# Queries of heads 0 to 13 computed with the keys and values, gates one head late, weight scaling on GpSimd

## The chip, the cores and the metric

The kernel runs on one core of a Trainium2 chip. The metric is the device time of one execution in microseconds (us). A core has a matrix engine (TensorE, PE in the profile; its weight loads are PEld), three engines that work element by element on 128 partitions (VectorE = DVE, ScalarE = ACT, GpSimd = POOL), a sync engine (SP) that issues most of the transfers, 16 DMA engines, an on-chip memory (SBUF) and the accumulators of TensorE (PSUM, eight banks here).

## The reference, cut to what matters

One inference step of an encoder over 640 tokens: 512 of one new stream, and 16 for each of 8 running streams. Layer A mixes and projects; then come shared keys and values, one layer B of attention, and a last norm. The part that matters, shortened:

```python
hk = rmsnorm(x, norm_kv)
kvf = hk @ w_kv                      # 2048 -> 2048 keys, 2048 values, 16 forget logits
k, v = kvf[..., :2048], kvf[..., 2048:4096]        # 16 heads of 128
h = rmsnorm(x, norm_b)
z = h @ w_in_b                       # 2048 -> 2048 queries, 2048 gates
q, gate = z[..., :2048], z[..., 2048:]
s = einsum(q, k_all) / sqrt(128) + Fq - Fk         # forgetting attention, causal
o = softmax(s) @ v_all
x = x + (o * silu(gate)) @ w_out_b
return rmsnorm(x, norm_f), k, v, ...
```

Both norms divide a row by the same root mean square and differ only in their gain per channel. All is float32; the kernel forms a large product of float32 from three matmuls on a high and a low part of each operand (high with high, high with low, low with high).

## The kernel before, in words

The stream lies transposed in SBUF, channels on partitions and the 640 tokens along the free axis, split into high and low parts.

**First part of layer B, the key and value stage** (`kv_pair`, L1034, called for the list `kvs` of L318). The list has 16 entries (q, m): q is 0 for keys and 1 for values, m counts pairs of heads. `pair8` (L260) computes one entry, 256 output channels, by a scheme that makes four block products out of seven (`ORDER`, L253, `OPER`, L119): over four slabs of weights (one entry of `loads` each, 512 KB) it issues 7 products x 2 x 3 = 42 matmuls of 128x320 a slab, 168 an entry. `advance` (L235) fetches and prepares slabs ahead: `prep` (L208) scales a slab by the norm gain on ScalarE (four instructions, L213), forms sums on VectorE and splits both into high and low. `combine` (L280) puts the seven products together on VectorE, GpSimd multiplies the pair by the row factors `R` (L1050), and `rows_out` (L1017) sends it on, as a generator that `tick` advances at some points of the next entry. Keys are stored transposed to the DRAM scratch `kscr` and row-wise to the output; values go row-wise to the scratch `sv`. The last entry takes its slabs in the order `LAST` and starts `last_blocks` (L1008).

**Second part, the attention loop** (from L1437). `proj` (L1132) computes 128 channels of the queries or gates of one head by eight plain block products for the pair of heads' seven: 16 steps of 6 matmuls of 128x320, 96 in all, on weights that `fetchb` loads in chunks of 256 KB (four a head) and `split_next` (L1110) scales (`scale_next`, L1104, on VectorE at L1107) and splits (L1115 on ScalarE, L1117 on VectorE). Between its steps it calls `step` (L1146), which advances two lists of generators in turn:

- `front` holds `scoring(h)`: transposes of the cached keys on VectorE (L1277), matmuls of scores (L1282 cached keys; L1290 and L1292 to L1294 new keys in four blocks), masks, softmax, and the loads and splits for the next head;
- `back` holds `valuing(h - 1)`: transposes of the probabilities (L105, through L1384 and L1385), products with the values (L1407, L1411, L1420 to L1423), and the output `og`.

`q_block` (L1223) runs `proj`, empties `front`, and writes the query of a head into SBUF (L1229 to L1232, then its split). `gate_block` (L1238) runs `proj`, applies `R` (L1241) and Silu, and hands the gate to `valuing`, which multiplies on GpSimd (L1434). Ahead of the loop stand `q_block(0)` and `q_block(1)`, the latter beside `scoring(0)`. A pass h of the loop, h = 1 to 15, puts `scoring(h)` and `valuing(h - 1)` on the lists and runs `gate_block(h - 1)` and `q_block(h + 1)`; pass 15 has no query block. `valuing(15)` with `gate_block(15)` follows, then the output projection and the last norm.

What sets the order: TensorE runs the matmuls in the order in which the program issues them (`manual_schedule`). The other engines' queues and SP's transfers are ordered by the framework's planner before the run, by its own estimate of when each instruction can go; on the chip each queue then runs in that fixed order, so that an instruction or a transfer that waits holds up all behind it. Every tile has a fixed number of buffers (`bufs`), and a load into a buffer waits for its last reader.

Of the kernel before, what the change touches and what calls it, by code (L numbers as in the profile page):

```python
# [39 lines left out]
def tile_yoco_step(ctx, tc, i, o):  # L40
# [167 lines left out]
    def prep():  # L208
        n = nprep[0]
        raw = loaded.pop(n)  # L210
        if len(loads[n]) > 2:
            for k in range(4):
                nc.scalar.activation(raw[:, k, :], raw[:, k, :], AF.Copy, scale=loads[n][2][:, k : k + 1])  # L213
# [104 lines left out]
    kvs = [(q, m) for m in range(8) for q in range(2)]  # L318
    LAST = (3, 0, 1, 2)
    for q, m in kvs:  # L320
        for s in LAST if (q, m) == kvs[-1] else range(4):
            c0 = q * D + m * 2 * P
            loads.append(("s", wkv[:, 4 * s : 4 * s + 4, c0 : c0 + 2 * P], nkv_c[:, 4 * s : 4 * s + 4]))
# [526 lines left out]
    kscr = [dram.tile([2 * P, NT], F32, name=f"kscr{m}") for m in range(8)]  # L850
    sv = [dram.tile([NT, P], F32, name=f"sv{h}") for h in range(H)]
# [11 lines left out]
    Fs = pv.tile([P, 5, H], F32, name="Fs")  # L863
    Fq, FqS = Fs[:, :4], Fs[:, 4]
# [152 lines left out]
    def rows_out(q, m, t):  # L1017
        yield
        if q == 0:
            store(pair_rows(kscr[m]), t)  # L1020
# [13 lines left out]
    def kv_pair(n, q, m):  # L1034
        def hook(s, j):
            if (n, s) == (0, 0) and j in (3, 6):
                last_forget(j // 6)
                if j == 6:
                    last_rows()
            if (n, s, j) == (15, 2, 0):  # L1040
                last_blocks()

        pp = pair8(hook, LAST if n == 15 else range(4))
# [60 lines left out]
    def scale_next(n):  # L1104
        if len(braws) > n and braws[n][1] is not None:
            r = braws[n][0].rearrange("p (k n) -> p k n", n=P)
            nc.vector.tensor_tensor(r, r, braws[n][1].unsqueeze(2).to_broadcast([P, 4, P]), op=ALU.mult)  # L1107
# [71 lines left out]
    with ExitStack() as ctx2:  # L1179
# [43 lines left out]
        def q_block(h):  # L1223
            pp = proj()
            drain(front)
            qt = pk.tile([P, NP], F32, tag="qt", name="qt")
            qs = pk.tile([P, NS], F32, tag="qs", name="qs")
            sc = float(P) ** -0.5
            nc.vector.scalar_tensor_tensor(qt[:, :HALF], pp[:, 0, :HALF], sc, R[:, :HALF], op0=ALU.mult, op1=ALU.mult)  # L1229
            nc.vector.scalar_tensor_tensor(qt[:, HALF:], pp[:, 1, : NP - HALF], sc, R[:, HALF:NP], op0=ALU.mult,  # L1230
                                           op1=ALU.mult)
            nc.vector.scalar_tensor_tensor(qs, pp[:, 1, NP - HALF : HALF], sc, R[:, NP:], op0=ALU.mult, op1=ALU.mult)  # L1232
            qh = pk.tile([P, NP], F32R, tag="qh", name="qh")
            ql = pk.tile([P, NP], F32R, tag="ql", name="ql")
            split(qh, ql, qt)
            return qt, qh, ql, qs

        def gate_block(h):  # L1238
            pp = proj(16 if h > H - 3 else 10)
# [3 lines left out]
            gates.append(sg)  # L1243
# [22 lines left out]
        cached, gates = {}, []  # L1266
# [3 lines left out]
        def scoring(h, q_):  # L1270
# [41 lines left out]
            qt, qh, ql, qs = q_  # L1312
            if h == 0:
                split_new_keys(0)
            kt, kh, kl = keys[h]
# [25 lines left out]
            nc.tensor.matmul(sn[:, :NS], qs, kt[:, NP:NT], start=True, stop=True)  # L1341
            nc.vector.scalar_tensor_tensor(s2[:, : 2 * PAST], ss, FqS[:, h : h + 1], fs[:, : 2 * PAST], op0=ALU.add,
# [16 lines left out]
            if more:  # L1359
                split_new_keys(h + 1)  # L1360
                load_sums(h + 1)
# [6 lines left out]
        def valuing(h):  # L1368
# [63 lines left out]
            while not gates:  # L1432
                yield
            nc.gpsimd.tensor_tensor(og[:, h, :], og[:, h, :], gates.pop(), op=ALU.mult)  # L1434
# [5 lines left out]
        load_new_keys(0)  # L1440
        load_sums(0)
        load_values(0)
        load_new_values(0)
        q_ = {}
        q_[0] = q_block(0)
        front.append(scoring(0, q_[0]))
        q_[1] = q_block(1)
# [139 lines left out]
```

## Time and profile before

| what | us |
| --- | --- |
| median of 3 runs | 2844.34 |
| lowest and highest | 2841.94, 2845.12 |
| the profiled execution, its own time | 2844.21 |
| its span, first to last instruction | 2842.5 |
| TensorE busy in the span | 2760.4 (97%) |
| VectorE busy | 2019.7 (71%) |
| ScalarE busy | 1151.2 (41%) |
| GpSimd busy | 404.8 (14%) |

The granted TensorE clock has a mean of 0.987 over the span. The span starts with layer A, up to about 1541 us; the key and value stage ends at 1951.7, the attention loop with its tail at about 2607, and the output projection fills the rest. Busy time is a share of the whole span; what an engine bounds is read stage by stage.

### The profile page before, as it was taken

Reading aid. Unit: us, or ns where it says so; the run is one execution under the profiler, and the core shown is the slowest. Engines: PE = TensorE matmul, PEld = TensorE weight load, DVE = VectorE, ACT = ScalarE, POOL = GpSimd, SP = SyncE. Lnnn points to the kernel's source line nnn. Section 1 sums busy time; section 2 is a strip of 40 time slices with the busy share of each in tenths; the row PEclk is TensorE's granted clock in tenths of the full one; section 3 lists DMA queues with packets and bytes.
Section 4 is the critical chain, followed back from the end, with each engine's and each line's share of the span. In section 5 each row is a group of like instructions: output and inputs, shape, how many; then the busy total and the mean of one; then the engine's idle time right before and its main releaser. Section 6 shows DMA issues by size and latency. Waiting matters only on the chain.

```text
span 2842.5 us, 46301 instructions
## 1 busy us (share of the span) xinstructions
PE 2760.4 (97%) x18194; PEld 2649.7 (93%) x18194; DVE 2019.7 (71%) x3415; ACT 1151.2 (41%) x1912; POOL 404.8 (14%) x373
## 2 busy tenths in 40 slices
PE   7899999999999999999998999998999999999998
PEld 7799999999998999999997999998999999998787
DVE  7877778888786858586365988886766766666333
ACT  5443333333333535343234555553434443444222
POOL 2212122232340120202023101111000000000000
PEclk8999999999999999999999999999999999999999
DMA  3344444444335686868642455556565655565832
GB/s 126 109 139 130 134 124 122 140 124 130 118 110 182 174 169 182 175 173 165 177 154 87 109 130 122 136 118 158 138 155 141 150 129 141 140 153 118 130 96 98
DMA packets 647044, 391.36 MB, mean 138 GB/s; under 512 B 322788, under 2 KB 601748, under 8 KB 646696
## 3 DMA queue, kind: packets, MB, share of 16 engines
q1 hardware_dynamic: 627240, 334.64, 44.1%
q0 software_dynamic: 19584, 53.75, 8.8%
q8 instruction: 142, 2.33, 0.3%
q14 instruction: 78, 0.64, 0.1%
HBM read 299.98 MB, written 88.32 MB: 137 GB/s over the span
## 4 chain that ended last, share of the span: by engine, by line
PE 43%; DVE 4%; DMA 2%; ACT 1%; issue 1%; POOL 1%; SPq 0%; DVEq 0%; ACTq 0%; POOLq 0%
PE banks L1086 15%; PE banks L251 9%; PE banks L1479 7%; PE banks L669 5%; PE banks L1407 2%; DVE wl L84 2%; PE banks L1282 1%; DMA raw<-in_w_kv 1%; PE banks L105 1%; ACT wh L81 0%; DMA raw<-in_w_grp_a 0%; PE banks L1422 0%; PE banks L1421 0%; PE banks L1420 0%; PE banks L1292 0%
## 5 line engine op out<-in xcount | busy, mean ns | idle before, releaser
L251 PE MATMUL banks<-b,wh 128*128 128x320 f32 x2688 | 605.1, 312 | 10.4 <-ACT forgot L840 6.6
L251 PE MATMUL banks<-th,wh 128*128 128x320 f32 x1792 | 559.8, 312 | 9.1 <-ACT cve L292 6.2
L251 PE MATMUL banks<-th,wl 128*128 128x320 f32 x1792 | 557.6, 311 | 4.0 <-DVE wl L84 4.0
L251 PE MATMUL banks<-tl,wh 128*128 128x320 f32 x1792 | 557.3, 311 | 0.7 <-DVE tl L84 0.7
L251 PEld LDWEIGHTS banks<-b,wh 128*128 128x128 f32 x2688 | 451.7, 189 | 12.3 <-ACT forgot L840 7.2
L251 PE MATMUL banks<-b,wl 128*128 128x320 f32 x1344 | 417.2, 310 | 0.4 <-DVE wl L84 0.4
L84 DVE TENSOR_TENSOR wl<-raw,wh 128x768 fp32r<-128x768 f32 (+1 forms) x264 | 307.4, 1165 | 145.0 <-ACT wh L81 144.5
L81 ACT ACTIVATE wh<-raw 128x768 fp32r<-128x768 f32 (+1 forms) x264 | 230.6, 875 | 379.9 <-issue 138.2
L81 ACT ACTIVATE wh<-sums 128x1024 fp32r<-128x1024 f32 x224 | 236.2, 1054 | 340.5 <-DVE sums L220 340.1
L1086 PE MATMUL banks<-b,whi 128*128 128x320 f32 x1536 | 355.4, 315 | 0.0
L251 PEld LDWEIGHTS banks<-th,wh 128*128 128x128 f32 x1792 | 339.7, 190 | 11.4 <-ACT cve L292 6.9
L251 PEld LDWEIGHTS banks<-th,wl 128*128 128x128 f32 x1792 | 339.7, 190 | 4.7 <-DVE wl L84 4.7
L251 PEld LDWEIGHTS banks<-tl,wh 128*128 128x128 f32 x1792 | 339.9, 190 | 1.0 <-DVE tl L84 1.0
L84 DVE TENSOR_TENSOR wl<-sums,wh 128x1024 fp32r<-128x1024 f32 x224 | 281.5, 1257 | 59.9 <-ACT wh L81 59.5
L1086 PEld LDWEIGHTS banks<-b,whi 128*128 128x128 f32 x1536 | 254.8, 189 | 1.6 <-issue 0.2
L251 PEld LDWEIGHTS banks<-b,wl 128*128 128x128 f32 x1344 | 253.9, 189 | 0.6 <-DVE wl L84 0.6
L1086 PE MATMUL banks<-b,wlo 128*128 128x320 f32 x768 | 196.1, 310 | 0.0
L217 DVE TENSOR_TENSOR sums<-raw 128x512 f32<-128x512 f32 x236 | 172.4, 730 | 14.6 <-DMA raw<-in_w_out_a 3.5
L1115 ACT ACTIVATE whi<-raw 128x512 fp32r<-128x512 f32 x144 | 90.0, 628 | 151.9 <-PE banks L1086 56.3
L669 PE MATMUL banks<-th,wh 128*128 128x320 f32 x576 | 132.3, 311 | 4.4 <-DVE cve L294 3.9
L1086 PEld LDWEIGHTS banks<-b,wlo 128*128 128x128 f32 x768 | 133.9, 188 | 0.0
L669 PE MATMUL banks<-tl,wh 128*128 128x320 f32 x576 | 131.8, 310 | 0.0
(397 smaller groups left out, 4830.6 us busy)
## 6 DMA issues: line engine op xcount, KB each, us to landing
raw<-in_w_in_a SPq DMA_DIRECT2D x128, 512.0 KB, 4.1
raw<-in_w_out_a SPq DMA_DIRECT2D x64, 512.0 KB, 4.9
raw<-in_w_kv SPq DMA_DIRECT2D x64, 512.0 KB, 3.9
raw<-in_w_in_b SPq DMA_DIRECT2D x128, 256.0 KB, 3.6
raw<-in_w_grp_a SPq DMA_DIRECT2D x32, 512.0 KB, 6.1
kc<-in_cache_k SPq DMA_DIRECT2D x64, 256.0 KB, 4.8
vc<-in_cache_v SPq DMA_DIRECT2D x16, 1024.0 KB, 6.7
raw<-in_w_out_b SPq DMA_DIRECT2D x64, 256.0 KB, 3.3
```

The costliest lines, as they stand in the source:

```text
L81: a = nc.scalar.activation(hi, x, AF.Copy)
L84: nc.vector.tensor_tensor(lo, x, hi.bitcast(F32), op=ALU.subtract)
L105: nc.tensor.transpose(out, x, ident[:n, :n])
L217: nc.vector.tensor_tensor(sums[:, :, 0:2, :], raw[:, :, 1:3, :], raw[:, :, 0:1, :].to_broadcast([P, 2, 2, P]), op=ALU.subtract)
L251: nc.tensor.matmul(bank[:, :HALF], w[kk][:, a, :], x, start=first and q == 0, stop=last and q == 2)
L669: nc.tensor.matmul(bk[s], w, x[:, s * HALF : (s + 1) * HALF], start=k + q == 0, stop=k == 7 and q == 2)
L1086: nc.tensor.matmul(acc_[:, s, :HALF], w, stream(k, q, s), start=f, stop=l)
L1115: nc.scalar.activation(hi, raw, AF.Copy)
L1282: nc.tensor.matmul(sp[rows, b % 2 * PAST : (b % 2 + 1) * PAST], qs[:, rows], kct[:, b * PAST : (b + 1) * PAST], start=True, stop=True)
L1407: nc.tensor.matmul(po[32 * q : 32 * q + 32, :P], pts[:, j, 32 * q : 32 * q + 32], vc[:, 4 * q + j, :], start=(j == 0), stop=False)
L1479: nc.tensor.matmul(out, (ol if q == 2 else oh)[k][:, ts], wl if q == 1 else wh, start=first and q == 0, stop=last and q == 2)
```

## The change

The query products of heads 0 to 13 move from the attention loop into the key and value stage, as seven more entries of `kvs` (q = 2). Their weights come from `w_in_b` and are scaled by a gain that already has the factor 1/sqrt(128) in it (`qgain`). The order at the end of the list becomes keys 6, values 6, keys 7, values 7, queries 6. A query pair takes the path of a key pair up to the factor `R` and goes, transposed, to a new DRAM scratch `qscr`; it has no row-wise output. Heads 14 and 15 keep their plain query blocks, which now stand ahead of the loop beside `scoring(0)`, with 6 steps each, and store to `qscr` as well.

In the loop `load_query(h + 1)` fetches a head's query (320 KB) during `scoring(h)`, and `split_query(h + 1)` splits it after the last score block of head h. A pass has one gate block with 22 steps, after which both lists are emptied; then the gate is taken from PSUM, and VectorE multiplies it into `og`. The scaling of the attention loop's weights goes from VectorE to GpSimd. `step` is called at evenly spread places of `proj`.

```diff
@@ prep
+            gain, k0 = qgain[0] if loads[n][2] == 2 else nkv_c, loads[n][3]
             for k in range(4):
-                nc.scalar.activation(raw[:, k, :], raw[:, k, :], AF.Copy, scale=loads[n][2][:, k : k + 1])
+                nc.scalar.activation(raw[:, k, :], raw[:, k, :], AF.Copy, scale=gain[:, k0 + k : k0 + k + 1])
@@ the list
-    kvs = [(q, m) for m in range(8) for q in range(2)]
+    kvs = [(q, m) for m in range(8) for q in range(3)]
+    kvs = kvs[:20] + kvs[21:23] + kvs[20:21]
+    qgain = []
...
+            loads.append(("s", (wkv, wkv, winb)[q][:, 4 * s : 4 * s + 4, c0 : c0 + 2 * P], q, 4 * s))
...
+    qgain.append(pv.tile([P, KT], F32, name="qg"))
+    nc.vector.tensor_scalar_mul(qgain[0], nb_c, float(P) ** -0.5)
@@ rows_out
-        if q == 0:
-            store(pair_rows(kscr[m]), t)
+        if q != 1:
+            store(pair_rows((kscr if q == 0 else qscr)[m]), t)
+        if q == 2:
+            return
@@ scale_next
-            nc.vector.tensor_tensor(r, r, braws[n][1].unsqueeze(2).to_broadcast([P, 4, P]), op=ALU.mult)
+            nc.gpsimd.tensor_tensor(r, r, braws[n][1].unsqueeze(2).to_broadcast([P, 4, P]), op=ALU.mult)
@@ proj
-                if kk * ticks % KT < ticks:
+                for _ in range((kk + 1) * ticks // KT - kk * ticks // KT):
                     step()
@@ queue of weight chunks
-    queue(winb, 0, nb_c)
-    queue(winb, P, nb_c)
+    for h in (14, 15):
+        queue(winb, h * P, nb_c)
     for h in range(H):
         queue(winb, D + h * P, nb_c)
-        if h < H - 2:
-            queue(winb, (h + 2) * P, nb_c)
@@ attention loop
+        def load_query(h):
+            qt = pk.tile([P, NT], F32, tag="qt", name="qt")
+            dma(qt, qscr[h // 2][h % 2 * P : (h % 2 + 1) * P, :])
+            queries[h] = [qt]
+
+        def split_query(h):
+            qh = pk.tile([P, NP], F32R, tag="qh", name="qh")
+            ql = pk.tile([P, NP], F32R, tag="ql", name="ql")
+            split(qh, ql, queries[h][0][:, :NP])
+            queries[h] += [qh, ql]
+
         def q_block(h):
+            pp = proj(6)
+            qp = pb.tile([P, NT], F32, tag="vt", name="qp")
+            nc.vector.scalar_tensor_tensor(halves(qp), pp[:, :, :HALF], float(P) ** -0.5, halves(R), op0=ALU.mult,
+                                           op1=ALU.mult)
+            dma(qscr[h // 2][h % 2 * P : (h % 2 + 1) * P, :], qp)
 
         def gate_block(h):
-            pp = proj(16 if h > H - 3 else 10)
+            pp = proj(22 if h < H - 1 else 12)
+            drain(front)
+            drain(back)
...
-            gates.append(sg)
+            nc.vector.tensor_tensor(og[:, h, :], og[:, h, :], sg, op=ALU.mult)
@@ scoring
+            if more:
+                load_query(h + 1)
...
                 split_new_keys(h + 1)
+                split_query(h + 1)
                 load_sums(h + 1)
@@ valuing
-            while not gates:
-                yield
-            nc.gpsimd.tensor_tensor(og[:, h, :], og[:, h, :], gates.pop(), op=ALU.mult)
+            finished.append(h)
@@ the loop
-        q_[0] = q_block(0)
-        front.append(scoring(0, q_[0]))
-        q_[1] = q_block(1)
+        front.append(scoring(0))
+        q_block(14)
+        q_block(15)
+        drain(front)
         for h in range(1, H):
-            front.append(scoring(h, q_[h]))
+            front.append(scoring(h))
             back.append(valuing(h - 1))
             gate_block(h - 1)
-            if h < H - 1:
-                q_[h + 1] = q_block(h + 1)
-            drain(front)
-            drain(back)
```

More of the change, by code (lines that the diff above doesn't have):

```diff
@@ L321, in tile_yoco_step @@
         for s in LAST if (q, m) == kvs[-1] else range(4):
-            c0 = q * D + m * 2 * P
-            loads.append(("s", wkv[:, 4 * s : 4 * s + 4, c0 : c0 + 2 * P], nkv_c[:, 4 * s : 4 * s + 4]))
+            c0 = q % 2 * D + m * 2 * P
+            loads.append(("s", (wkv, wkv, winb)[q][:, 4 * s : 4 * s + 4, c0 : c0 + 2 * P], q, 4 * s))
     start = ExitStack()
@@ L850, in tile_yoco_step @@
     kscr = [dram.tile([2 * P, NT], F32, name=f"kscr{m}") for m in range(8)]
+    qscr = [dram.tile([2 * P, NT], F32, name=f"qscr{m}") for m in range(8)]
     sv = [dram.tile([NT, P], F32, name=f"sv{h}") for h in range(H)]
@@ L1039, in hook @@
                     last_rows()
-            if (n, s, j) == (15, 2, 0):
+            if (n, s, j) == (len(kvs) - 1, 2, 0):
                 last_blocks()
-        pp = pair8(hook, LAST if n == 15 else range(4))
+        pp = pair8(hook, LAST if n == len(kvs) - 1 else range(4))
         if n == 0:
@@ L1221, in tile_yoco_step, with q_block @@
         nc.gpsimd.memset(fs[:, : 2 * PAST], -NEG)
-        def q_block(h):
-            pp = proj()
-            drain(front)
[L1226 to L1232, printed above, removed]
+        queries = {}
+        def load_query(h):
[3 more added lines that the diff above has]
+        def split_query(h):
             qh = pk.tile([P, NP], F32R, tag="qh", name="qh")
             ql = pk.tile([P, NP], F32R, tag="ql", name="ql")
-            split(qh, ql, qt)
-            return qt, qh, ql, qs
+            split(qh, ql, queries[h][0][:, :NP])
+            queries[h] += [qh, ql]
+        def q_block(h):
+            pp = proj(6)
[3 more added lines that the diff above has]
+            dma(qscr[h // 2][h % 2 * P : (h % 2 + 1) * P, :], qp)
         def gate_block(h):
-            pp = proj(16 if h > H - 3 else 10)
+            pp = proj(22 if h < H - 1 else 12)
+            drain(front)
+            drain(back)
             sg = pb.tile([P, NT], F32, tag="vt", name="sgb")
@@ L1264, in load_values, with scoring @@
             cached[h].append(vc)
-        cached, gates = {}, []
+        cached, finished = {}, []
         scores = {}
-        def scoring(h, q_):
+        def scoring(h):
             more = h < H - 1
@@ L1311, in scoring @@
             yield
-            qt, qh, ql, qs = q_
             if h == 0:
                 split_new_keys(0)
+                split_query(0)
+            qt, qh, ql = queries[h]
+            qs = qt[:, NP:]
             kt, kh, kl = keys[h]
@@ L1440, in tile_yoco_step @@
         load_new_keys(0)
+        load_query(0)
         load_sums(0)
@@ L1443, in tile_yoco_step @@
         load_new_values(0)
-        q_ = {}
-        q_[0] = q_block(0)
-        front.append(scoring(0, q_[0]))
-        q_[1] = q_block(1)
+        front.append(scoring(0))
+        q_block(14)
+        q_block(15)
+        drain(front)
         for h in range(1, H):
-            front.append(scoring(h, q_[h]))
+            front.append(scoring(h))
             back.append(valuing(h - 1))
             gate_block(h - 1)
-            if h < H - 1:
-                q_[h + 1] = q_block(h + 1)
-            drain(front)
-            drain(back)
         back.append(valuing(H - 1))
         gate_block(H - 1)
-        drain(back)
     ordered.close()
```

## The prediction

> **What bounds the kernel now.** I read the table of stages first (busy time of each engine in stretches between boundaries found in the timeline). Columns: stretch and length, then busy time and instruction count of PE, PEld, DVE, ACT and POOL, granted clock, DMA share, GB/s.
>
> ```profile
> core 0: us, PE busy (x) PEld busy (x) DVE busy (x) ACT busy (x) POOL busy (x), PEclk, DMA share, GB/s
> 1672.00:1848.00 176.00, 176.00 (x1202) 176.00 (x1201) 151.39 (x209) 100.59 (x179) 21.22 (x7) 1.00 0.54 129
> 1951.70:1995.40 43.70, 35.54 (x228) 33.22 (x228) 27.90 (x55) 11.24 (x21) 3.17 (x2) 0.92 0.78 184
> 1995.40:2556.40 561.00, 560.08 (x3945) 519.46 (x3944) 379.80 (x819) 231.87 (x465) 21.72 (x14) 1.00 0.57 143
> 2556.40:2583.20 26.80, 26.13 (x188) 23.13 (x187) 20.98 (x46) 11.75 (x23) 0.33 (x1) 1.00 0.34 89
> 2583.20:2607.00 23.80, 21.81 (x160) 20.05 (x158) 15.66 (x28) 16.46 (x34) 1.57 (x1) 1.00 0.31 92
> ```
>
> The rows are the key and value stage in its steady part, the entry to attention, passes 1 to 14 of the head loop, pass 15, and the last gate. TensorE is busy throughout both large stages (176.00 of 176.00, 560.08 of 561.00), so both are bound by the number of matmuls. One matmul of 128x320 takes 176.00 / 1202 = 0.146 us, and passes 1 to 14 take 561.0 / 14 = 40.07 us each.
>
> Pass 15 matters most. It is the one pass without a query block: scoring of head 15, valuing of head 14, one gate block. Its two ends, on VectorE (the last query block is taken from PSUM) and TensorE (first matmul of gate 15):
>
> ```profile
> 2556.42 0.49 DVE L1229 SCALAR_TENSOR_TENSOR qt<-banks,R 128x320 f32<-128x320 f32 x1 [2.13 <-PE banks L1086]
> 2583.18 0.39 PE L1086 MATMUL banks<-th,whi 128*128 128x320 f32 x1
> ```
>
> It took 26.8 us. So the trace already holds one pass of the kind that the change makes of all fifteen.
>
> The steady pace of the key and value stage comes from its last combining step (an entry's last VectorE subtraction or addition), by the view of that line between 1675 and 1955:
>
> ```profile
> L286 DVE TENSOR_TENSOR x<-cu,banks x12: 476/482/489, 1680.8 to 1951.8; 128x320 f32<-128x320 f32 x12
> ```
>
> Twelve entries, eleven intervals: (1951.8 - 1680.8) / 11 = 24.64 us an entry, which is 168 matmuls at 0.146 us and nothing else.
>
> **The change part by part.** *Removed from the loop:* 14 query blocks. By matmuls alone that is 14 x 96 x 0.1464 = 197 us. What is lost with them is filler between steps that wait for other engines, so I count by passes: 14 passes of 40.07 us become 14 of the kind of pass 15, 14 x (40.07 - 26.80) = 185.8 us less. Pass 15 and the last gate stay as they are.
>
> *Added in the key and value stage:* seven entries of 24.64 us, 172.5 us more. A query pair goes through the same preparation, combining and factor multiply as a key pair, and VectorE is busy for 151.39 of 176.00 us there; it lacks the two row-wise transposes and their stores. The store to the scratch is one transfer on SP, like that of the keys. I count these at nothing beside TensorE's 24.64 us.
>
> So the two large terms nearly cancel: -185.8 + 172.5 = -13.3 us. All hangs on whether a pass really takes 26.8 us, for 0.9 us a pass is the whole gain. Three things differ from pass 15.
>
> *VectorE's load.* Passes 1 to 14 have 379.80 / 14 = 27.13 us of VectorE a pass. These groups go or change (line, operation, shapes, count | busy us, mean ns | idle before):
>
> ```profile
> L1117 DVE TENSOR_TENSOR wlo<-raw,whi 128x512 fp32r<-128x512 f32 x112 | 76.3, 681 | 3.7 <-ACT whi L1115 2.4
> L1107 DVE TENSOR_TENSOR raw<-raw,cols 128x512 f32<-128x512 f32 x112 | 74.9, 680 | 0.0
> L1229 DVE SCALAR_TENSOR_TENSOR qt<-banks,R 128x320 f32<-128x320 f32 x14 | 6.9, 491 | 27.2 <-PE banks L1086 27.2
> L1230 DVE SCALAR_TENSOR_TENSOR qt<-banks,R 128x192 f32<-128x192 f32 x14 | 4.9, 348 | 0.0
> L1232 DVE SCALAR_TENSOR_TENSOR qs<-banks,R 128x128 f32<-128x128 f32 x14 | 3.9, 281 | 0.0
> L1241 DVE TENSOR_TENSOR sgb<-banks,R 128x640 f32<-128x640 f32 x14 | 11.5, 825 | 20.0 <-PE banks L1086 20.0
> ```
>
> Eight scalings (8 x 0.680), four low parts (4 x 0.681) and the query's three instructions (0.491 + 0.348 + 0.281) go, 9.3 us; the gate's multiply comes over from GpSimd, about 0.83 us by the row of the same 640 elements (estimate). 27.1 - 9.3 + 0.8 = 18.7 us. Pass 15 has 20.98 us, so VectorE has no more to do than in the pass that I take as the model.
>
> *GpSimd's scaling, four chunks of 512 elements a pass.* No row shows that; the nearest are
>
> ```profile
> L1434 POOL TENSOR_TENSOR og<-og,sgb 128x640 f32<-128x640 f32 x16 | 25.2, 1576 | 631.2 <-ACT og L1431 579.1 <-DVE pr L1304 28.9 <-ACT sgb L1242 23.1
> L1050 POOL TENSOR_TENSOR x<-x,R 128x1280 f32<-128x1280 f32 x16 | 48.8, 3052 | 333.7 <-DVE x L286 290.1 <-DMA out_k_sample<-kn 43.7
> ```
>
> On the line through both, 512 elements take about 1.28 us (estimate), 5.1 us a pass, on an engine that is otherwise idle there. The chunks are prepared three ahead of use, so their own latency is covered by some 20 us. What GpSimd does to VectorE is another matter (the timeline; the same VectorE instruction with and without GpSimd beside it):
>
> ```profile
> 1681.46 3.02 POOL L1050 TENSOR_TENSOR x<-x,R 128x1280 f32<-128x1280 f32 x1 [21.83 <-DVE x L286]
> ...
> 1681.58 3.72 DVE L84 TENSOR_TENSOR wl<-raw,wh 128x768 fp32r<-128x768 f32 x1
> ...
> 1688.60 0.95 DVE L84 TENSOR_TENSOR wl<-raw,wh 128x768 fp32r<-128x768 f32 x1
> ```
>
> The subtraction waited 2.8 us, until GpSimd's multiply had ended. [...]
>
> *The wait for the cached keys.* Pass 15 has one wait within it, and this is its place:
>
> ```profile
> 2560.00 0.38 PE L105 MATMUL banks<-ident,pr 128*128 128x128 f32 x2
> 2561.93 1.64 PE L1282 MATMUL banks<-kct,qs 128*32 128x256 f32 x8 [0.67 <-DVE kct L1277]
> ...
> 2572.64 1.06 PE L1282 MATMUL banks<-kct,qs 128*32 128x256 f32 x8
> ...
> 2560.84 0.42 DVE L1385 TENSOR_TENSOR ptl<-banks,pth 128x256 fp32r<-128x256 f32 x1 [1.80 <-ACT pth L1384]
> 2561.18 1.29 DVE L1277 STREAM_TRANSPOSE kct<-kc 128x512 f32<-128x512 f32 x2
> ```
>
> VectorE stood idle for 1.80 us, yet its queue had the transposes of the cached keys behind a subtraction that waited for TensorE and ScalarE. TensorE lost 0.67 us ahead of the eight matmuls and 1.64 - 1.06 = 0.58 us among them. With 22 steps instead of 16 the steps lie closer, yet these two (the second transpose of probabilities and the first scores) keep one step of projection between them, six matmuls. I leave the 1.25 us as they are; without them a pass would take 26.80 - 1.25 = 25.55 us.
>
> *The entry to attention.* Scoring of head 0 now begins within the first query block, at the third of six steps, 8 x 6 x 0.146 = 7.0 us after its first matmul; before, it came after a whole block.
>
> ```profile
> 1957.44 0.63 PE L1086 MATMUL banks<-th,whi 128*128 128x320 f32 x1 [5.66 <-ACT whi L1115]
> 1977.55 1.06 PE L1282 MATMUL banks<-kct,qs 128*32 128x256 f32 x8
> ...
> 1956.18 2.06 SPq L870 DMA_DIRECT2D sv<-kn  x4
> 1962.09 3.26 SPq L870 DMA_DIRECT2D sv<-kn  x4
> 1965.95 4.96 SPq L1259 DMA_DIRECT2D kc<-in_cache_k  x4
> ```
>
> The key loads were issued 8.5 us after the first matmul, and the first scores ran 20.1 us after it. If nothing moved, TensorE would wait for them, up to about 10 us with the issue (4.96), the landing (about 5) and the transposes. But SP's two groups of value stores (2.06 + 3.26 us and what they waited for) belong to the last entry, which is now a query pair with one store; the loads can go some 5 us sooner. And the 5.66 us of idle TensorE may shrink by up to 3, as its weights then wait behind fewer transfers. Between -3 and +10; I take +3. The tail after pass 15 I leave alone (0, bounds -2 and +2, its idle time being 23.80 - 21.81).
>
> *Sum:* -185.8 + 172.5 + 3 = -10.3 us on the profiled execution's 2844.21, which lies 0.13 us under the median of the runs: 2833.9, so **2834 us** for the median.
>
> **The rivals.**
>
> *The key transposes come free (faster still).* With eight scalings gone from its queue VectorE may turn the keys earlier. For: its 1.80 us of idleness just there. Against: the order is the planner's, and passes 1 to 14 had the same wait in the same place. Fifteen passes of 25.55: 15 x 1.25 = 19 us less, **2815**.
>
> *GpSimd holds VectorE up on the path (slower).* Place: the four scalings of each pass. A scaling that starts just ahead of a low part or a mask on which TensorE's next step hangs costs up to 1.28 us each time. [...] One full meeting a pass on the path is 15 x 1.28 = 19 us, **2853**. It decides from 10.3 / 15 = 0.7 us a pass on. [...] For: the 3.72 us above. Against: VectorE keeps 5 us of slack in a 26.8 us pass.
>
> *The keys come late (slower).* SP issues one pass's loads in a fixed order (start, duration on SP's queue):
>
> ```profile
> 2529.68 0.34 SPq L1259 DMA_DIRECT2D kc<-in_cache_k  x1
> 2537.87 0.37 SPq L1101 DMA_DIRECT2D raw<-in_w_in_b  x1
> 2538.29 3.51 SPq L1259 DMA_DIRECT2D kc<-in_cache_k  x3
> ```
>
> The second to fourth key loads stood 7.9 us behind a weight load that waited for its buffer. In a 40 us pass that is harmless. In a 26.8 us pass the loads go out from about 11 us on; held as long, they land near 11 + 8 + 4 + 5 = 28, 1 us into the next pass, and are wanted 4.8 us into it (2561.18 - 2556.42). Held 6 us longer they cost about 2 us a pass, 30 us, **2864**. Against: half the weight loads are gone.
>
> *The seven products bring nothing (slower).* If the new entries ran at the price of what they replace, 2 x 96 x 0.146 = 28.1 us, then 7 x 3.5 = 24 us more, **2858**. For: VectorE's 86% in that stage. Against: twelve entries at TensorE's own pace.
>
> **How the numbers follow.** Forecast (passes like pass 15, the entry between its bounds): 0.50, its own range 2828 to 2841. Free transposes 0.12, GpSimd on the path 0.25, late keys 0.08, no gain from the products 0.05. A measurement of this kernel can tell about 0.2%, 5.7 us, so faster means under 2838.6 and slower over 2850.0. Faster: 0.40 of the forecast's 0.50, and the 0.12. Same: the other 0.10, and 0.08 of GpSimd's case where the meetings are partial. Slower: 0.17 + 0.08 + 0.05. The range 2814 to 2858 leaves out the late keys, the worst of GpSimd's case and a little below.
>
> **What would show it.** Right: query entries at 24.6 us; passes of 26 to 27.5 us; one short wait of TensorE a pass, for the key transposes. Wrong: VectorE instructions of two SBUF inputs over 1.5 us long beside GpSimd's scaling with TensorE waiting behind them; key transposes idle until a transfer lands; a wait of over 6 us early in the first query block. The forecast fails most easily by the length of a pass, of which each 0.4 us is 6 us.

## The result, and the profile after

The changed kernel takes **2873.04 us**, median of four runs (2869.47 to 2876.82), beside 2843.14 for the kernel before on the same chip: a ratio of 1.0102, 95% interval 1.0089 to 1.0115. It is 1% slower, where 2834 (0.3% faster) was predicted. The profiled execution took 2869.47 us with a span of 2867.7, 25.3 us over the 2844.21 that the prediction's sum was made against. By stages:

| stage | before, us | after, us | difference | predicted |
|---|---|---|---|---|
| up to the K/V stage | 1550.5 | 1546.3 | -4.2 | 0 |
| K/V stage, 16 entries, then 23 | 401.2 | 590.6 | +189.4 | +172.5 |
| entry to the head loop | 43.7 | 50.4 | +6.7 | +3 |
| passes 1 to 15 | 587.8 | 421.6 | -166.2 | -185.8 |
| last gate and output | 259.3 | 258.8 | -0.5 | 0 |

The first stage is the same code in both kernels, and its end wanders by several microseconds between runs (by the same wait in it, from 1538.0 to 1547.4 in the runs below), so experiments are compared stage by stage. One of the six executions of the kernel with both orders, below, took 6293.67 us for a reason that no trace shows; its numbers are of the other five.

Below are busy times by stretch of the changed kernel (columns as in the prediction: stretch, length, busy time of PE, PEld, DVE, ACT, POOL, granted clock, DMA share, GB/s): the K/V stage from its steady part on, the entry, passes 1 to 14.

```profile
1672.00:2136.90 464.90, 456.67 (x3061) 452.98 (x3059) 375.34 (x514) 248.63 (x440) 55.44 (x23) 0.99 0.47 117
2136.90:2187.30 50.40, 37.38 (x223) 34.98 (x223) 25.03 (x47) 12.69 (x25) 18.12 (x16) 0.83 0.77 192
2187.30:2580.85 393.55, 368.62 (x2606) 325.90 (x2605) 274.56 (x614) 189.97 (x403) 59.93 (x57) 1.00 0.71 177
```

In the K/V stage TensorE was busy for all of its stretch before (176.00 of 176.00). Now it lacks 8.2 of 464.9 us, and its clock is not full throughout (0.99 granted over the stretch). In the passes it lacks 24.9 of 393.6 us, 1.8 a pass, though VectorE has 274.56 / 14 = 19.6 us of work in a pass of 28.1. No engine became the bound: in both stages TensorE waits for something that is small and late.

**A pass.** First TensorE where it stops once a pass, then VectorE's queue at that place and one row of ScalarE, each row with its start, its duration and the idle time ahead of it.

```profile
2245.79 0.45 PE L1094 MATMUL banks<-b,wlo 128*128 128x320 f32 x2
2248.09 1.64 PE L1295 MATMUL banks<-kct,qt 128*32 128x256 f32 x8 [1.85 <-DVE kct L1290]
```

```profile
2242.49 0.82 DVE L1254 TENSOR_TENSOR sgb<-banks,R 128x640 f32<-128x640 f32 x1
2243.22 1.22 DVE L1125 TENSOR_TENSOR wlo<-raw,whi 128x512 fp32r<-128x512 f32 x1
2245.45 0.83 DVE L1256 TENSOR_TENSOR og<-og,sgb 128x640 f32<-128x640 f32 x1 [1.01 <-ACT sgb L1255]
2246.20 0.61 DVE L1403 TENSOR_TENSOR ptl<-banks,pth 128x128 fp32r<-128x128 f32 x2
2246.73 0.68 DVE L1125 TENSOR_TENSOR wlo<-raw,whi 128x512 fp32r<-128x512 f32 x1
2247.33 1.30 DVE L1290 STREAM_TRANSPOSE kct<-kc 128x512 f32<-128x512 f32 x2
```

```profile
2246.05 0.63 ACT L1123 ACTIVATE whi<-raw 128x512 fp32r<-128x512 f32 x1 [0.18 <-PE banks L1094]
```

The first scores wait 1.85 us for the key transposes and then run at their pace (1.64 us for eight matmuls that take 1.06). The transposes are last in a row of VectorE work that begins with the gate's eviction. Right ahead of them stands a wlo; it needs ScalarE's whi, and whi had to wait for projection matmuls of the same pass, right ahead of the scores. From the start of the last of these to the scores it is 2248.09 - 2245.79 = 2.30 us. The keys had landed long before; SP issued their loads here, and the page has 4.7 us from issue to landing for them:

```profile
2223.04 5.01 SPq L1272 DMA_DIRECT2D kc<-in_cache_k  x4
```

**The K/V stage.** The same view as the prediction's, the last combining step of each entry, now with nineteen entries of steady state:

```profile
L287 DVE TENSOR_TENSOR x<-cu,banks x19: 478/483/489, 1677.4 to 2137.0; 128x320 f32<-128x320 f32 x19
```

(2137.0 - 1677.4) / 18 = 25.53 us an entry, where 24.64 was predicted. It is uneven: the starts within one round of three lie 23.4, 28.9 and 24.7 us apart (1756.12, 1779.51, 1808.43 and 1833.13 in the timeline), the long one at the key entry that follows an entry of queries. TensorE stands still there, and ScalarE shows why:

```profile
1804.64 0.41 PE L252 MATMUL banks<-th,wh 128*128 128x320 f32 x1 [1.97 <-ACT cve L293]
...
1805.97 0.46 PE L252 MATMUL banks<-th,wh 128*128 128x320 f32 x1 [0.20 <-DVE cu L294]
1806.23 0.47 PE L252 MATMUL banks<-tl,wh 128*128 128x320 f32 x1
```

```profile
1797.30 0.89 ACT L214 ACTIVATE raw<-raw,cols 128x256 f32<-128x256 f32 x2
1801.28 1.31 ACT L214 ACTIVATE raw<-raw,cols 128x256 f32<-128x256 f32 x3 [3.08 <-DMA raw<-in_w_kv]
1802.49 0.83 ACT L81 ACTIVATE wh<-raw 128x768 fp32r<-128x768 f32 x1
1803.22 1.04 ACT L81 ACTIVATE wh<-sums 128x1024 fp32r<-128x1024 f32 x1
1804.17 0.41 ACT L293 ACTIVATE cve<-banks 128x320 f32<-128x320 f32 x1
```

The copy cve, which frees a PSUM bank for the next entry, ran at 1804.17, last behind a scaling that waited 3.08 us for its load. The loads in turn went out one at a time. SP's row, VectorE's rows, and the page's row for these loads (count, size, us to landing):

```profile
1791.03 6.80 SPq L185 DMA_DIRECT2D raw<-in_w_kv  x2
```

```profile
1790.05 0.96 DVE L84 TENSOR_TENSOR wl<-raw,wh 128x768 fp32r<-128x768 f32 x1 [1.74 <-ACT wh L81]
...
1796.48 0.96 DVE L84 TENSOR_TENSOR wl<-raw,wh 128x768 fp32r<-128x768 f32 x1 [2.61 <-ACT wh L81]
```

```profile
raw<-in_w_kv SPq DMA_DIRECT2D x64, 512.0 KB, 3.8
```

Each load was issued at the moment at which a low part (wl) ended, 1791.03 behind 1790.05 + 0.96, and again 6.4 us later behind 1796.48 + 0.96. So there is a loop: wl frees a raw buffer, the load into it takes 3.8 us, a scaling of it runs on ScalarE, and only behind that scaling stands the wh of another slab, for which the next wl waits. 3.8 + 0.9 + 0.83 + 0.96 = 6.5 us a slab, where TensorE uses one up in 24.64 / 4 = 6.16 us. The two rounds seen here took 6.4 us (the two ends of wl above) and 6.9 (the next load went out at 1804.34).

### The profile page after: what moved, and what is told of

Same layout as the page of the kernel before. It is cut to its first block, busy times and chain, and to the rows that moved or that the text cites. A ratio compares the mean times of both kernels' runs of the same rounds, so it can differ in the third digit from the quotient of the medians.

```text
span 2867.7 us, 46347 instructions
## 1 busy us (share of the span) xinstructions
PE 2750.6 (96%) x18026; PEld 2631.8 (92%) x18026; DVE 2049.8 (71%) x3391; ACT 1208.2 (42%) x2029; POOL 477.8 (17%) x436
## 4 chain that ended last, share of the span: by engine, by line
PE 33%; DVE 7%; DMA 5%; ACT 4%; issue 2%; POOL 1%; SPq 0%; DVEq 0%; ACTq 0%; POOLq 0%
PE banks L252 8%; PE banks L1491 8%; PE banks L1094 6%; PE banks L672 5%; DMA raw<-in_w_kv 3%; DVE wl L84 3%; PE banks L1425 2%; PE banks L1295 2%; ACT wh L81 1%; ACT raw L214 1%; PE banks L105 1%; DVE x L287 1%; ACT L1255 0%; DVE sums L220 0%; DVE sums L218 0%
## 5 line engine op out<-in xcount | busy, mean ns | idle before, releaser
L252 PE MATMUL banks<-b,wh 128*128 128x320 f32 x3024 | 680.7, 312 | 10.6 <-ACT forgot L843 6.7
L252 PE MATMUL banks<-th,wh 128*128 128x320 f32 x2016 | 632.2, 314 | 17.4 <-ACT cve L293 13.1
L252 PE MATMUL banks<-th,wl 128*128 128x320 f32 x2016 | 629.0, 312 | 3.9 <-DVE wl L84 3.9
L252 PE MATMUL banks<-tl,wh 128*128 128x320 f32 x2016 | 628.5, 312 | 0.7 <-DVE tl L84 0.7
L1094 PE MATMUL banks<-b,whi 128*128 128x320 f32 x864 | 200.6, 316 | 0.0
L1058 POOL TENSOR_TENSOR x<-x,R 128x1280 f32<-128x1280 f32 x23 | 70.0, 3044 | 498.0 <-DVE x L287 474.8
L1094 PEld LDWEIGHTS banks<-b,whi 128*128 128x128 f32 x864 | 146.7, 192 | 1.6
L214 ACT ACTIVATE raw<-raw,cols 128x256 f32<-128x256 f32 x256 | 111.9, 498 | 82.9 <-DMA raw<-in_w_kv 73.5
L1115 POOL TENSOR_TENSOR raw<-raw,cols 128x512 f32<-128x512 f32 x72 | 76.5, 1065 | 371.8 <-DMA raw<-in_w_in_b 326.8
L221 DVE TENSOR_TENSOR sums<-raw,sums 128x256 f32<-128x256 f32 x264 | 133.1, 504 | 5.8
L672 PE MATMUL banks<-th,wh 128*128 128x320 f32 x576 | 131.9, 310 | 2.1 <-DVE cve L295 1.6
```

The source lines that it names most:

```text
L221: nc.vector.tensor_tensor(sums[:, :, 3, :], raw[:, :, 3, :], sums[:, :, 2, :], op=ALU.subtract)
L252: nc.tensor.matmul(bank[:, :HALF], w[kk][:, a, :], x, start=first and q == 0, stop=last and q == 2)
L672: nc.tensor.matmul(bk[s], w, x[:, s * HALF : (s + 1) * HALF], start=k + q == 0, stop=k == 7 and q == 2)
L1058: nc.gpsimd.tensor_tensor(t, t, R.unsqueeze(1).to_broadcast([P, 2, NT]), op=ALU.mult)
L1094: nc.tensor.matmul(acc_[:, s, :HALF], w, stream(k, q, s), start=f, stop=l)
L1115: nc.gpsimd.tensor_tensor(r, r, braws[n][1].unsqueeze(2).to_broadcast([P, 4, P]), op=ALU.mult)
```

## Experiments

All edits are to the changed kernel. The order in which an engine issues its instructions is planned from estimates of when each is ready; `tc.issue_after(x)` holds what is traced in its block behind x on x's engine, and `tc.keep_in_program_order(a)` keeps `a` behind what is traced ahead of it. In the long lists "..." stands for lines left out.

### The length of a pass

Two theories to begin with: the multiply of the gate, now on VectorE, stands ahead of the keys (A), or GpSimd's scaling holds VectorE up (B). Three single edits.

**Keys traced first.** The generator of the next head's scoring is started at the end of a pass.

```diff
             drain(back)
+            if h < H - 2:
+                keys_ahead(h + 2)     # runs scoring(h + 2) up to its second transpose
             sg = pb.tile([P, NT], F32, tag="vt", name="sgb")
```

> The first two key transposes of the next head are issued before the gate is taken from PSUM at the end of the pass, the rest as in the changed kernel. Theory A (a pass of 28.06 us is long because VectorE's queue has the gate's chain - its copy from PSUM, the wait for Silu and its table load, the multiply into the output - ahead of the key transposes, and TensorE waits for these): the wait of 1.83 us ahead of the first scores and the 0.58 us among them go, passes of about 25.7 us, the whole run about 2838 us. Theory B (GpSimd's scaling holds VectorE up): passes stay within 0.5 us of 28.06.

2871.26 us, passes of 28.04 to 28.07 but for one of 29.90 and one of 29.42, the wait 1.85 as before. VectorE's issue order had not changed, so the run tells nothing of either theory.

**The gate's multiply back on GpSimd.**

```diff
-            nc.vector.tensor_tensor(og[:, h, :], og[:, h, :], sg, op=ALU.mult)
+            nc.gpsimd.tensor_tensor(og[:, h, :], og[:, h, :], sg, op=ALU.mult)
```

> The gate's multiply goes back to GpSimd, the scaling stays there. Theory A: VectorE loses 1.01 us of idleness behind Silu and 0.83 us of work ahead of the key transposes, the wait falls to about 0.3 us, passes of about 26.5 us, run about 2850. Theory B: GpSimd has 1.6 us more a pass to hold VectorE up with, passes of 28.1 us or longer.

2885.69 us; the wait grew to 2.04 us, and passes came in turns of 28.2 and 29.8. The multiply alone is not the cause. The passes are as long as B expected; what grew is the wlo right ahead of the transposes, which took 0.89 us beside GpSimd's work instead of 0.68.

**The scaling back on VectorE.**

```diff
-            nc.gpsimd.tensor_tensor(r, r, braws[n][1]...
+            nc.vector.tensor_tensor(r, r, braws[n][1]...
```

> The scaling of the gate weights goes back to VectorE, the gate's multiply stays there too. Theory A: VectorE has 2.4 us more to do and the wait for the key transposes stays or grows, passes of 28.0 to 28.8 us. Theory B: no GpSimd work beside VectorE in the loop, no VectorE instruction over its undisturbed duration, passes at least 1 us shorter, 27 us or less.

2879.28 us, wait 2.01, passes of 28.2 and 29.8 in turns. Theory B falls: without GpSimd's scaling the passes are no shorter. VectorE has the scalings to do here, so this alone does not clear GpSimd; the last run of this section does, which keeps the scaling on GpSimd and has no wait.

**Keys first, with the gate's eviction pinned behind them** (with the edit of the first run).

```diff
-            nc.vector.tensor_tensor(halves(sg), pp[:, :, :HALF], ...
+            a = nc.vector.tensor_tensor(halves(sg), pp[:, :, :HALF], ...
+            tc.keep_in_program_order(a)       # behind the transposes traced above
```

> The first two key transposes of the next head stand ahead of the gate's eviction and multiply in VectorE's queue, this time pinned. Theory A (VectorE's queue at the start of a pass holds the key transposes): the 1.85 us wait of the first score matmuls goes, as 2.66 us (eviction 0.82, idle for the Silu 1.01, multiply 0.83) no longer stand ahead; passes of 25.6 to 26.4 us instead of 28.06, the run 24 to 36 us shorter than the changed kernel. Rival B (the keys themselves, or a lock of GpSimd, are late): passes stay at 27.5 to 28.1. Rival C (the bank of the gate that is now emptied later is wanted): a new wait of 1 to 2 us for L1267 in each pass, passes 27 to 28.

**Only the multiply, pinned behind the second key transpose.**

```diff
-            nc.vector.tensor_tensor(og[:, h, :], og[:, h, :], sg, op=ALU.mult)
+            gated.append((h, sg))
...
             turn_keys(kct, 0, 1)
+            gate_rows(True)                   # the multiply, kept behind the transposes
```

> The gate's eviction stays where it is; only its multiply goes behind the next head's first two key transposes in VectorE's queue. Theory A: 1.84 us (idle for the Silu 1.01 and multiply 0.83) no longer stand ahead of the keys, so the wait of 1.85 us goes to 0.0 to 0.5 and a pass takes 26.2 to 26.8 us. Rival B (keys or GpSimd late): passes stay at 27.5 to 28.1. If the wait here is as short as with the eviction moved too, the idle for the Silu is the main part.

Both missed in full: 2876.03 and 2873.04 us, passes of 28.05, wait 1.83. Theory A as first put is dead, since 2.66 and 1.84 us of work and waiting had left the place ahead of the keys. The rows of the run with the pinned eviction show what filled it:

```profile
2392.41 0.69 DVE L1125 TENSOR_TENSOR wlo<-raw,whi 128x512 fp32r<-128x512 f32 x1 [0.28 <-ACT whi L1123]
2394.16 0.29 DVE L1418 TENSOR_TENSOR ptl<-banks,pth 128x128 fp32r<-128x128 f32 x1 [1.05 <-ACT pth L1417]
2395.36 0.42 DVE L1418 TENSOR_TENSOR ptl<-banks,pth 128x256 fp32r<-128x256 f32 x1 [0.92 <-ACT pth L1417]
2396.25 0.69 DVE L1125 TENSOR_TENSOR wlo<-raw,whi 128x512 fp32r<-128x512 f32 x1 [0.46 <-ACT whi L1123]
2396.86 1.30 DVE L1305 STREAM_TRANSPOSE kct<-kc 128x512 f32<-128x512 f32 x2
```

```profile
2395.33 0.45 PE L1094 MATMUL banks<-b,wlo 128*128 128x320 f32 x2
2395.59 0.63 ACT L1123 ACTIVATE whi<-raw 128x512 fp32r<-128x512 f32 x1 [0.26 <-PE banks L1094]
2397.62 1.64 PE L1310 MATMUL banks<-kct,qt 128*32 128x256 f32 x8 [1.83 <-DVE kct L1305]
```

The planner still put the transposes behind two ptl and a wlo, and VectorE was idle for 1.05 + 0.92 + 0.46 us ahead of these, since they hang, through ScalarE's pth and whi, from matmuls of the new pass. The chain from the projection matmuls through whi and wlo to the transposes and the scores takes 2397.62 - 2395.33 = 2.29 us, as the 2.30 of the changed kernel, which is why the wait stood still whatever left the rows ahead. These 2.43 us of idle time of VectorE are no sign of slack, as the instruction that TensorE needs stands behind them. Theory A2: not what is ahead of the keys counts, but whether anything there is released only by TensorE in the same pass.

**All early work of the next pass held behind the keys.**

```diff
+            behind = ExitStack()
+            if held and c == 0:               # first quarter of a gate block
+                behind.enter_context(tc.issue_after(held[0]))   # the second key transpose
             wh, wl = (w.rearrange("p (k n) -> p k n", n=P) for w in chunk())
```

> The first two key transposes of the next head are traced at the end of a pass, and what VectorE does in the next pass's first quarter is held behind them. In the two runs before, the wait stood unchanged at 1.83 us: there the transposes came behind a wlo that waits for whi, which waits for a bank pass of TensorE in the new pass itself. Theory A2 (VectorE's order: the transposes behind operations that TensorE releases only after the pass began): the wait goes, passes of 25.6 to 26.4 us, the run 25 to 36 us below the changed kernel. Rival B (the keys themselves come late): the wait stays at 1 to 1.9 us, passes 27.2 to 28.1. Rival D (the Silu and multiply, now ahead of the first wlo, delay weights): a new wait for wlo, passes 26.5 to 28.

2856.61 us: the wait is down to 0.71, a pass to 26.93, above A2's 25.6 to 26.4. The planner put the transposes behind the gate's multiply this time, and that waits for the Silu. A wait for weights, rival D's mechanism, did not come.

**The same, with the multiply behind the keys too.**

> As the run beside it, with the gate's multiply behind the key transposes too: the transposes come right behind the last normalization of a pass, ahead of the gate's eviction. Theory A2: wait gone, passes of 25.6 to 26.2 us. Rival B: passes 27.2 to 28.1 as before. Rival D does not apply here, since the multiply no longer stands ahead of wlo: if this run is shorter than the one beside it by more than 0.3 us a pass, D was part of it.

**2836.62 us**, every pass from the second on 25.56 or 25.57 from first scores to first scores. VectorE and TensorE at the start of a pass:

```profile
2371.80 0.49 DVE L1350 TENSOR_SCALAR pr<-pr,rw 128x512 f32<-128x512 f32 x1
2372.20 1.30 DVE L1321 STREAM_TRANSPOSE kct<-kc 128x512 f32<-128x512 f32 x2
2373.42 1.65 DVE L1271 TENSOR_TENSOR og<-og,sgb 128x640 f32<-128x640 f32 x1
```

```profile
2375.50 0.45 PE L1094 MATMUL banks<-b,wlo 128*128 128x320 f32 x2
2375.89 1.06 PE L1328 MATMUL banks<-kct,qt 128*32 128x256 f32 x8
```

The transposes follow the last normalization of the old pass; the scores wait for nothing and take 1.06 us. A2 is shown: the same instructions in another order give 28.06 - 25.57 = 2.49 us a pass, the 1.85 ahead of the scores and the 0.58 among them. Of these, 1.36 us a pass (26.93 - 25.57) is the Silu and multiply. GpSimd's scaling is still there and still holds VectorE up: the multiply took 1.65 us instead of 0.83, beside a scaling of GpSimd at 2373.36, and TensorE did not wait.

### The pace of the K/V stage

**The copy of m1 on VectorE.** Theory K: ScalarE's queue holds cve behind scalings of late slabs.

```diff
-        nc.scalar.activation(v, pp["m1"][:, :HALF], AF.Copy)
+        nc.vector.tensor_copy(v, pp["m1"][:, :HALF])        # in the K/V stage
```

> In the 23 entries of the K/V stage the copy of m1 out of PSUM is on VectorE instead of ScalarE. Theory K (ScalarE's queue holds this copy behind the scalings of a weight slab that landed late): the TensorE waits of about 2 us for the copy go, the stage takes 573 to 579 us instead of 590.6 (23 entries at before's 24.64 plus the 7 us that before had beside them). Rival L (the slabs themselves come too slowly, one load at a time at 6.7 to 7 us against TensorE's 6.16): TensorE waits for split weights instead, stage 586 to 592. The passes stay at 28.06.

Between the two: 2866.47 us, the stage 6.2 us shorter (1540.17 to 2138.24 between two waits that every run has at its ends, for forgot and for the first whi: 598.1 us, against 604.3 in the changed kernel). The waits for cve are gone, and waits of 0.44 to 1.14 us for cu of VectorE took their place. cve was where it showed, not where it arose.

**Query entries last.**

```diff
-    kvs = [(q, m) for m in range(8) for q in range(3)]
+    kvs = [(q, m) for m in range(8) for q in range(2)] + [(2, m) for m in range(7)]
```

> The seven query entries run after all sixteen key and value entries instead of between them. Theory K with the mix as its trigger (an entry of queries, 23.4 us, leaves the slabs behind and the key entry after it pays): key and value entries take before's 24.6 each, and the query entries among themselves drift: 16 x 24.64 + 7 x 24.6 + 7 = 574 to 580. Rival L (any stretch in which an entry has no stores and takes 23.4 us outruns the loads): the seven query entries show waits of TensorE of 1 to 2 us each, stage 583 to 592. Rival M (the query slabs are no slower than others; only the order of three is bad): no wait at all, 7 x 23.4, stage 565 to 573.

2870.87 us, the stage 603.0 against 604.3 by the same two marks: rival L's figure. TensorE waits 1.07 to 2.33 us in each of five entries, all in the row of query entries at the end. The mix of the three kinds is not the cause. What it is in a query entry that tips ScalarE's order is not shown.

**Each slab's scalings behind the copies (wh) of the slab before.**

```diff
+            with tc.issue_after(wholes[-1]):                # wh of the slab before
                 for k in range(4):
                     nc.scalar.activation(raw[:, k, :], raw[:, k, :], AF.Copy, ...
```

> On ScalarE the four scalings of a weight slab are held behind the rounding copies (wh) of the slab before it; in the changed kernel up to 7 scalings, those of the next slab and some of the one after, stand ahead of a slab's wh. Theory O (ScalarE's order closes a loop: the product wl of slab n-1 frees a buffer, the load into it takes 3.8 us, a scaling of 0.5 to 0.9 waits for it, and only then come wh of slab n, 0.83, and wl, 0.96: 6.5 us and more for a slab that TensorE uses up in 6.16): the waits for cve go, the key entries after a query take 24.6 instead of 29, and the stage takes 573 to 578 us instead of 590.6. Rival L (the loads themselves cannot come faster): stage 584 to 592, TensorE waits for split weights or for cve. Passes stay at 28.06; the run 2856 to 2862.

**2851.01 us**; the stage takes 587.8 by the same marks, 16.5 us less, and no wait of TensorE is left in its steady part. The kernel before took 415.1 us between these marks (1542.32 to 1957.44); with the 172.5 us forecast for the seven entries that makes 587.6. The combining step again, and ScalarE's order:

```profile
L292 DVE TENSOR_TENSOR x<-cu,banks x19: 486/489/490, 1676.9 to 2120.4; 128x320 f32<-128x320 f32 x19
```

```profile
1789.90 1.69 ACT L218 ACTIVATE raw<-raw,cols 128x256 f32<-128x256 f32 x4
1793.81 0.85 ACT L81 ACTIVATE wh<-raw 128x768 fp32r<-128x768 f32 x1 [2.22 <-PE banks L257]
1794.57 1.04 ACT L81 ACTIVATE wh<-sums 128x1024 fp32r<-128x1024 f32 x1
1795.51 0.42 ACT L298 ACTIVATE cve<-banks 128x320 f32<-128x320 f32 x1
```

(2120.4 - 1676.9) / 18 = 24.64 us an entry, keys, values and queries alike. The scalings no longer wait for loads; wh now waits for TensorE, which is the right way round. Rival L falls: nothing about the loads was changed but the time at which their buffers came free. Both fixes agree: order alone gave 2.49 us a pass and 16.5 us the stage.

### The entry, and both orders together

**Scoring of head 0 stepped only in the second query block** (0 steps in the first, 10 in the second).

```diff
-            pp = proj(6)
+            pp = proj(0 if h == 14 else 10)
```

> All steps of head 0's scoring go into the second query block (ten steps), none into the first. If the 7.5 us wait for the loaded query in the entry is the loads' time from the end of the stage before, it goes: the entry falls from 50.4 to 43 to 44 us and the run by about 7 us, 2866. If the loads are only asked for later as well, it moves into the second block and the entry stays within 2 us of 50.4. The passes stay at 28.06 us in either case.

2872.24 us, not 2866: the entry took 45.5 instead of 50.4, with a wait of 2.75 us for wlo in the second block, and a wait of 2.98 us for qt came up in the first pass, so 3.1 net.

**Both orders together** (the edits of the two bold results above).

> The scalings held behind the copies (K/V stage) and the key transposes with the gate's multiply behind them (passes), together. If the two causes are separate and add up: K/V stage 574 us (-16.5), 14 passes of 25.57 instead of 28.06 (-35) and the one of 29.9 gone (-2), tail +0.7: 2873 - 53 = 2820, range 2815 to 2826, a ratio of 0.990 to 0.994 to the kernel before. If they share a cause or one brings the other's wait back: 2830 or more.

**2817.17 us**, ratio to the kernel before 0.9917 (0.9904 to 0.9930). That is 55.9 us below the changed kernel, 53 expected: the two causes add up. K/V entries at 24.64 us and passes at 25.57 stand in its trace as in the single runs.

**On top of it, 0 and 14 steps at the entry; or, instead, qt's load ahead of the keys' loads.**

```diff
-        load_keys(0)
-        load_new_keys(0)
         load_query(0)
+        load_keys(0)
+        load_new_keys(0)
```

> As the combination, with head 0's scoring stepped only in the second of the two query blocks at the entry (none in the first, 14 in the second). Theory S (the entry's excess is SP's queue: four weight loads and the cached keys' loads, 5.1 and 6.0 to 6.5 us of issue, stand ahead of the load of qt that the first scores wait for, and stepping the scores 24 us later hides it): the qt wait goes, the entry takes 44 to 46 us instead of 50.4, and the later load of the next head's qt costs 0 to 2 in the first pass: 3 to 6 us below the combination. Rival W (the entry's excess is the first weight copies, 5.5 us): the entry shrinks by less than 2.

> As the combination, with the load of head 0's qt issued ahead of the cached keys' four loads instead of behind them. Theory S, in its narrow form (only qt's own place in SP's queue): the wait for qt of 7.1 to 9.5 us is cut by the 6 to 8 us that the keys' issues take, the entry 44 to 46. Rival T (the cached keys land as late as qt, and their transposes are waited for next): a wait for kct of 5 to 8 us takes its place, and the time is within 1.5 us of the combination.

The 14 steps: **2814.01 us**, ratio 0.9900 (0.9888 to 0.9913); from the entry's first wait to pass 2 it takes 69.2 us against 73.1 in the combination, 3.8 less. qt first: 2818.51, 1.3 more and so no change. In the combination the first scores waited 7.78 us for qt; with qt first, their wait and VectorE's key transposes are:

```profile
2147.76 2.51 PE L1333 MATMUL banks<-kct,qt 128*32 128x256 f32 x8 [8.27 <-DVE kct L1326]
```

```profile
2146.99 1.30 DVE L1326 STREAM_TRANSPOSE kct<-kc 128x512 f32<-128x512 f32 x2 [3.88 <-DMA kc<-in_cache_k]
```

The cached keys are as late as qt, so rival T holds: what the first scores need is issued on SP in one row, and of what was tried only asking later helped. What stays open is a remaining wait of 4.32 us for the next qt with 14 steps, and the idle time ahead of the first weights, 5.50 us in every run here but the one with the scaling on VectorE (1.84 for whi and 2.50 for wlo there), which was not followed up.

## Why the prediction was wrong, point by point

- **What bounds the kernel.** Right in kind, wrong in what follows from it. TensorE busy for 176.00 of 176.00 us was taken to mean that the stage had room; it did not show how near ScalarE's order already was to the loop above. The trace of before has it: six scalings in a row ahead of a wh, and four more that wait for a load, though TensorE did not wait there.

```profile
1790.61 2.50 ACT L213 ACTIVATE raw<-raw,cols 128x256 f32<-128x256 f32 x6
1795.22 1.71 ACT L213 ACTIVATE raw<-raw,cols 128x256 f32<-128x256 f32 x4 [0.44 <-DMA raw<-in_w_kv]
```

- **"Passes 1 to 14 become 14 of the kind of pass 15": the step that cost most.** -185.8 was forecast and -166.2 came, a miss of 19.6. The mean pass is 28.1 us, not 26.8: 1.25 us in each of fourteen, 17.5, and about 1.9 more in one whose clock dropped (0.73 granted from 2278 to 2283 us). The step within it that failed is "I leave the 1.25 us as they are": it took the wait, and the place of the key transposes in VectorE's queue, over from pass 15. That the second transposes of probabilities and the first scores keep one step of projection between them was right. In pass 15 before, the scores were due 2561.93 - 0.67 - 2560.00 = 1.26 us after these transposes; in the pass of the changed kernel shown above it is 2248.09 - 1.85 - 2244.99 = 1.25:

```profile
2244.99 0.38 PE L105 MATMUL banks<-ident,pr 128*128 128x128 f32 x2
```

  But the key transposes, which in pass 15 stood right behind a ptl and started at 2561.18, 1.18 us after the mark, now stand behind a wlo too and start at 2247.33, 2.34 us after it. These 1.16 us make up the growth of the wait from 0.67 to 1.85. The prediction also said that passes 1 to 14 had the same wait in the same place; that holds for VectorE's idle time, while TensorE waited for the key transposes in one of them only (0.92 us in the first). So the trace of before did not show a constant.
- **VectorE's load.** Right: 18.7 us a pass were forecast, or 23.8 with the estimated 5.1 of GpSimd's scaling in full on top, and 19.6 came. But it was the wrong quantity. The order within the queue decided, not its sum.
- **GpSimd's scaling.** The price was 1.28 us, 1.04 came. All of them in the passes, and the one beside the wlo shown above:

```profile
L1115 POOL TENSOR_TENSOR raw<-raw,cols x59: 1039/1041/1209, 2190.0 to 2587.9; 128x512 f32<-128x512 f32 x59
```

```profile
2242.85 1.04 POOL L1115 TENSOR_TENSOR raw<-raw,cols 128x512 f32<-128x512 f32 x1 [6.51 <-DMA raw<-in_w_in_b]
```

  GpSimd does hold VectorE up: wlo at 2243.22, beside that scaling, took 1.22 us, and 0.68 at 2246.73 with no scaling beside it. The rival built on this came near the right length of a pass for a wrong reason: taking the scaling off GpSimd did not shorten the passes.
- **Seven entries at 24.64 us, preparation "at nothing beside TensorE".** A miss of 16.9 us, the second large one. TensorE's work in an entry was right to the hundredth, as 24.64 came back once ScalarE was reordered. What failed is the cover: the price of a query entry's preparation was not in its amount but in a plan that let scalings of slabs still under way stand ahead of finished ones. In part the waits cost twice: of TensorE's four waits for cve (1.97, 1.04, 1.97 and 2.14 us) all but the shortest were followed by a stretch at a lower clock (0.79, 0.79 and 0.83 granted in the 8 to 10 us around them, 1.00 around the shortest).
- **The entry.** +3 was taken out of -3 to +10, +6.7 came, and with it a wait of over 6 us early in the first query block, which the prediction had named as a sign of being wrong. TensorE's two waits and SP's key loads:

```profile
2142.42 0.64 PE L1094 MATMUL banks<-th,whi 128*128 128x320 f32 x1 [5.50 <-ACT whi L1123]
...
2159.54 1.93 PE L1295 MATMUL banks<-kct,qt 128*32 128x256 f32 x8 [7.52 <-DMA qt<-qscr]
```

```profile
2147.05 6.31 SPq L1272 DMA_DIRECT2D kc<-in_cache_k  x4
```

  The loads of the keys went out 4.6 us after the first matmul (2147.05 against 2142.42) instead of 8.5, so 3.9 us sooner where some 5 were hoped for. The idle time ahead of the first weights did not shrink (5.50 against 5.66), and the first scores waited 7.52 us, for the loaded query qt, which had no term in the sum.
- **The rivals.** "Key transposes come free" was wrong of the changed kernel and right of what it could do: 25.55 us a pass was worked out there, and 25.57 is what the reordered queue gives. "Keys late" was wrong: they landed at about 2228.05 + 4.7 = 2232.8 and were turned at 2247.33. "Seven products bring nothing" had the stage 24 us longer, where 16.9 came, but products were not the cause.
- **The sum.** The stage's 16.9, the passes' 19.6 and the entry's 3.7, less the 4.7 of the two stages that the change leaves alone, make 35.5 us: to 0.1 us the distance between the -10.3 forecast and the +25.3 of the profiled execution.

## What to carry to other kernels

A wait copied from a model pass is not a constant: when the work around it changes, find what the waiting instruction stands behind in its queue, and what releases that. A queue with idle time in it is no proof of slack: VectorE idled for 2.43 us here ahead of rows that the key transposes stood behind, while TensorE waited 1.83 us for these. Before adding work to a stage that a busy engine bounds, follow one buffer round (freed, loaded, scaled, copied, freed) and compare the round's length with the pace, 6.5 against 6.16 us here; where a plan puts work that waits, for a load or for the pass to come, ahead of work that is ready, holding it back cost no instruction and gave 55.9 us in this kernel.

## What the runs showed of the hardware that was not expected

After some waits of about 2 us TensorE ran at nearly half its pace for some 3 us. Behind the wait of 1.97 us at 1804.64 above, matmuls from 1805.97 on are 0.266 us apart instead of 0.146, thirteen of them; the granted clock in that stretch and around it:

```profile
1804.00:1810.00 6.00, 5.17 (x23) 4.91 (x24) 5.43 (x12) 2.85 (x7) 0.96 (x1) 0.72 0.28 87
1805.97:1809.16 3.19, 3.19 (x12) 3.19 (x13) 3.19 (x8) 1.02 (x3) 0.12 (x1) 0.54 0.39 132
```

That is about 1.6 us more for a wait of 2. The wait's length alone does not decide it: with the scaling on VectorE each pass waited 2.01 us and every second one was slowed (28.23 and 29.79 us in turns), waits of 1.85 us mostly did nothing but were followed by a slow pass twice (29.44 with the query entries last, 29.42 with the keys traced first), and of three waits of 2.12 two were followed by a pass of 29.9 and one by 28.34. What else decides it, no run here isolates.
